# Pinning every instruction of a planned recurrence to the order in which its planner emitted it

## The chip, the cores and the metric

The kernel runs on one core of one Trainium2 chip. The metric is the device time of the program in microseconds (us), lower is better. One core has TensorE (PE, matmuls; PEld are its weight loads), VectorE (DVE), ScalarE (ACT), GpSimd (POOL) and SyncE (SP), which here issues the DMAs. Each engine takes its instructions from one queue of its own, one after the other; an instruction that needs something from another engine waits on a semaphore at the head of its queue.

## The reference

A two-layer backbone over 512 latent tokens with 256 context tokens ahead of them, model width 1024. Layer 0 mixes with mLSTM and gated linear attention, layer 1 with a bidirectional RWKV-7, and each layer ends in a gated convolutional FFN. The part of the kernel that the change touches is the RWKV-7 mixing:

```python
def rwkv_project(h, shifted, mu, w_rkv, ...):
    xx = shifted - h
    xr, xw, xk, xv, xa, xg = (h + xx * mu[i] for i in range(6))
    r = xr @ w_rkv[0];  k = xk @ w_rkv[1];  v = xv @ w_rkv[2]
    ...
def step(S, inp):                       # one token of one head, 64x64 state
    rt, wt, kt, vt, kkt, at = inp
    sa = einsum("bhvk,bhk->bhv", S, -kkt)
    S = S * wt[:, :, None, :] + sa[..., None] * (kkt * at)[:, :, None, :] + vt[..., None] * kt[:, :, None, :]
    return S, einsum("bhvk,bhk->bhv", S, rt)
```

16 heads of 64 channels, 768 tokens, once forward and once backward; the latent scan starts from the state that the context left.

## The kernel before, in words

Up to line 1309 `rwkv_mixer` projects v, the low-rank terms and r on TensorE, in three products of split operands each (`dense`: weight high half by token high half, high by low, low by high). From line 1314 on `self.nc` is a `Meter`, and all that follows to line 1427 is emitted through it. This stretch is called the recurrence here.

Its work is cut into threads, each a Python generator:

- `kp0` to `kp7` (line 1273, called K0 to K7 below) are the eight output blocks of the k projection. They begin with eight rounds in which DVE makes `vt`, ACT casts it to `vh` and DVE subtracts for `vl` (the token halves; line 1275), then `unit` loads a block's weights (`wraw`, a DMA), ACT casts them to `whi` and DVE (even blocks) or POOL (odd ones) subtracts for `wlo` (lines 1277 and 1280, one block ahead). The products are `pk`; ACT copies them to `pv`, and a DMA stores them to `dk`.
- `shared p` (line 1438) prepares pair p of heads: it loads `k`, `v`, `r` and makes `kk`, `a`, `P0`, `P1` and the bonus `bv`; its products are `pn`, `pa`, `pkb`, `pbo`.
- A unit u is one pair in one direction (16 units, u = 2p and 2p + 1). `prep` (line 1571; `pw`, then `ps`) makes the decays and the chunk products `T1`, part of which goes through DRAM (`dx`). `leaf` (line 1712) loads it back and inverts 16x16 triangles by 30 short DVE instructions in a row, stores the result (`dqi`) and loads it as `q0t`. `feed` (line 1660, `ps`) and `values` (line 1685, `pvt`) prepare operands.
- `trans` (line 1744, three per unit) are dense products on `q0t` and `T1`: `pmg`, `pmy`, `pmt`, with ACT and DVE copies between.
- `rec` (line 1821) is the serial chain: 11 steps, each two `cst` products, then one `SU` on ACT and one on DVE, which the next step needs; then 16 `yps` products.
- `close` finishes a pair. `wo` (line 1395) starts the output projection for the first six pairs, block m = 0 to 7, and `fill` (`mod_fill`) makes eight blocks of the modulation vectors; both are there to be put between the rest. Their products are `wo` and `mfill`.

`flow` (line 214) decides in which order the threads emit: it keeps a time for each thread, takes the earliest, lets it emit to its next `yield`, and the `Meter` reckons from its own table of costs (line 180), its record of which buffers are written and read, and the time at which each engine is free, when that piece ends. PSUM banks are handed out the same way. So the order of emission is a list schedule by the `Meter`'s costs.

That order is not yet the order of the queues. The kernel is built in a tile framework whose scheduler goes over all instructions of the program, in order of emission as priority, with a cost model of its own: where it reckons that the next instruction of an engine isn't ready, it issues a later one that is. It may also move an instruction of the recurrence ahead of earlier parts of the program. Instructions are recorded at one line, 210, since all pass through `MeterEngine.call`; the tile names tell them apart.

Of the kernel before, what the change touches and what calls it, by code (L numbers as in the profile page):

```python
# [102 lines left out]
class Meter:  # L103
# [2 lines left out]

    SEM = 0.1

    def __init__(self, nc):
        self.nc, self.eng, self.mode = nc, {}, None  # L110
        self.free = dict(tensor=0.0, vector=0.0, scalar=0.0, gpsimd=0.0, sync=0.0)
        self.wr, self.rd = {}, {}
        self.avail = dict(L=[0.0] * 2, C=[0.0] * 2, R=[0.0] * 4)
        self.begin()
# [4 lines left out]
    def __getattr__(self, name):  # L119
        if name in self.free:  # L120
            return self.eng.setdefault(name, MeterEngine(self, name))
        return getattr(self.nc, name)
# [77 lines left out]
class MeterEngine:  # L200
# [3 lines left out]
    def __getattr__(self, op):  # L204
        f = getattr(getattr(self.meter.nc, self.name), op)

        def call(*a, **k):
            aps = [x for x in list(a) + list(k.values()) if isinstance(x, bass.AP)]
            self.meter.record(self.name, op, aps[0], aps[1:])
            return f(*a, **k)  # L210
        return call


# [57 lines left out]
class Net:  # L271
# [954 lines left out]
    def rwkv_mixer(self, hf, xd, norms=None, post=lambda *a: None):  # L1226
        nc, I = self.nc, self.I
# [83 lines left out]
        small = (uw, ua, ug, blk, half)  # L1311
        st = [dict(dirs=[{}, {}], ys=[None]) for _ in range(NC)]
        zh, zl, y = [None] * NC, [None] * NC, []
        meter = self.nc = Meter(nc)
        zero = self.sl("zero", 780)
        nc.gpsimd.memset(zero, 0.0)

# [755 lines left out]
```

## Time and profile before

| | |
|---|---|
| median of 3 runs | 2827.05 us (2825.29 to 2833.61) |
| the profiled execution | 2823.43 us, span 2821.7 us |
| mean granted TensorE clock | 0.937 |
| busy share of the span | PE 90%, DVE 57%, ACT 37%, POOL 39% |
| recurrence, first to last instruction of PE | about 1462 to 2357 us of the span |

"Busy" is the union of an engine's instructions. A view by windows gives the busy time of each engine in a stretch, the granted clock (1.00 is full) and the number of instructions. In a timeline a row has start, duration, engine, line, operation, tiles, shapes, and in brackets how long the engine had been idle and what it had waited for. The view of waits lists who waited for whom, with total, times and longest.

### The profile page before, as it was taken

What the parts mean: (1) busy time and instruction counts of PE and PEld (TensorE: products, weight loads), DVE (VectorE), ACT (ScalarE), POOL (GpSimd) and SP (SyncE); (2) the same over time, 40 slices, a digit from 0 to 9 for tenths busy, and PEclk for the clock granted to TensorE, in tenths of its full rate; (3) what the DMA queues carried; (4) which work ended last, traced back from release to release, by engine and by line L of the source; (5) the groups of instructions that cost most, each with busy time, mean ns of one, the idle gap of its engine ahead of it and who ended that gap; (6) DMA issues with size and microseconds to landing.
All of it is one profiled execution on the core that took longest, in us unless ns stands there. A gap on an engine that the chain in (4) does not pass through costs nothing.

```text
span 2821.7 us, 47085 instructions
## 1 busy us (share of the span) xinstructions
PE 2543.4 (90%) x19012; PEld 2064.8 (73%) x19012; DVE 1599.1 (57%) x2855; ACT 1056.2 (37%) x2205; POOL 1089.5 (39%) x1115
## 2 busy tenths in 40 slices
PE   5889999888899999986998969989998898989997
PEld 2677777778788888886766756767776677877777
DVE  4567756635535364457464265765666635555655
ACT  4543433445333232233442223434433334343332
POOL 2443445445333333435212133333323214464544
PEclk8999999989999999997999989999998998999999
DMA  6222233342121212221342222223122123232222
GB/s 225 67 83 74 64 131 120 111 142 83 49 63 55 63 56 68 75 98 59 113 134 73 88 63 55 75 61 76 47 57 47 33 73 120 71 95 81 90 77 97
DMA packets 186194, 233.59 MB, mean 83 GB/s; under 512 B 110840, under 2 KB 126584, under 8 KB 185976
## 3 DMA queue, kind: packets, MB, share of 16 engines
q1 hardware_dynamic: 185976, 230.58, 27.1%
q8 instruction: 149, 2.44, 0.4%
q14 instruction: 69, 0.57, 0.1%
HBM read 201.03 MB, written 29.51 MB: 82 GB/s over the span
## 4 chain that ended last, share of the span: by engine, by line
PE 27%; DVE 12%; DMA 4%; issue 3%; ACT 3%; POOL 2%; SPq 0%; POOLq 0%; DVEq 0%; ACTq 0%
DVE fa L1085 6%; PE pmg L210 4%; PE pmy L210 2%; PE ps L210 2%; PE pmt L210 2%; DVE leaf L210 2%; PE pk L210 2%; PE mfill L210 2%; PE cst L210 2%; PE wo L210 1%; PE pdL L373 1%; PE pdL L377 1%; PE pdL L374 1%; DMA wraw<-in_down 1%; POOL wlo L362 1%
## 5 line engine op out<-in xcount | busy, mean ns | idle before, releaser
L362 POOL TENSOR_TENSOR wlo<-wraw,whi 128x512 fp32r<-128x512 f32 (+1 forms) x469 | 643.3, 1388 | 836.7 <-ACT whi L361 667.8
L1085 DVE SCALAR_TENSOR_TENSOR fa<-pl,vec,fa 128x512 f32<-128x512 f32 x352 | 352.0, 1013 | 287.2 <-ACT fa L1083 276.4
L361 ACT CAST whi<-wraw 128x512 fp32r<-128x512 f32 (+1 forms) x529 | 296.9, 599 | 426.8 <-DMA wraw<-in_up 189.7
L210 POOL TENSOR_SCALAR_AFFINE_SELECT T<-T 64x256 f32<-64x256 f32 x192 | 100.7, 528 | 119.3 <-ACT T L210 72.1
L373 PE MATMUL pdL<-gh,whi 128*128 128x512 f32 x288 | 116.0, 403 | 16.4 <-DVE y L1142 11.6
L373 PE MATMUL pjL<-zh,whi 128*128 128x512 f32 x304 | 120.5, 396 | 4.6 <-DVE fa L1088 4.6
L373 PE MATMUL pjL<-mh,whi 128*128 128x512 f32 x304 | 120.6, 397 | 1.5 <-DVE fa L1088 1.5
L374 PE MATMUL pjL<-ml,whi 128*128 128x512 f32 x304 | 120.9, 398 | 0.0
L374 PE MATMUL pdL<-gl,whi 128*128 128x512 f32 x288 | 115.4, 401 | 5.9 <-POOL gl L1103 3.1
L374 PE MATMUL pjL<-zl,whi 128*128 128x512 f32 x304 | 120.6, 397 | 0.0
L377 PE MATMUL pjL<-mh,wlo 128*128 128x512 f32 x304 | 120.4, 396 | 0.0
L377 PE MATMUL pjL<-zh,wlo 128*128 128x512 f32 x304 | 119.8, 395 | 0.0
L1086 ACT ACTIVATE fa<-fa 128x256 f32<-128x256 f32 (+1 forms) x66 | 36.9, 560 | 213.6 <-DVE fa L1085 213.5
L377 PE MATMUL pdL<-gh,wlo 128*128 128x512 f32 x288 | 115.2, 400 | 0.0
L210 PE MATMUL pmy<-T,q0t 64*64 64x192 f32 x768 | 101.7, 360 | 1.2 <-DVE kk L210 0.8
L210 POOL TENSOR_TENSOR rn<-rn,powc 128x12 f32<-128x12 f32 (+1 forms) x16 | 31.3, 1959 | 180.5 <-DVE rn L210 169.8
L1142 DVE TENSOR_TENSOR y<-y,pdL 128x512 f32<-128x512 f32 x48 | 32.8, 686 | 111.9 <-PE pdL L377 111.9
L210 DVE TENSOR_SCALAR SU<-cst,el 64x64 f32<-64x64 f32 x176 | 51.1, 291 | 78.4 <-PE cst L210 73.3
L373 PE MATMUL pjC<-mh,whi 128*128 128x256 f32 x304 | 86.0, 283 | 9.5 <-DVE fa L1088 9.5
L210 ACT ACTIVATE SU<-cst,el 64x64 f32<-64x64 f32 x176 | 54.2, 308 | 106.2 <-PE cst L210 104.4
L210 ACT COPY T<-pmy 128x384 f32<-128x384 f32 x96 | 44.7, 477 | 115.2 <-PE pmy L210 106.0
L374 PE MATMUL pjC<-ml,whi 128*128 128x256 f32 x304 | 85.5, 281 | 0.0
(501 smaller groups left out, 7458.5 us busy)
## 6 DMA issues: line engine op xcount, KB each, us to landing
wraw<-in_up SPq DMA_DIRECT2D x88, 512.0 KB, 3.6
wraw<-in_wmod SPq DMA_DIRECT2D x64, 512.0 KB, 4.2
wfill<-in_wmod SPq DMA_DIRECT2D x32, 512.0 KB, 4.5
wraw<-in_rkv SPq DMA_DIRECT2D x24, 512.0 KB, 4.0
wraw<-in_win_fm SPq DMA_DIRECT2D x21, 512.0 KB, 3.9
wraw<-in_down SPq DMA_DIRECT2D x32, 320.0 KB, 2.9
xd<-y SPq DMA_DIRECT2D x64, 128.0 KB, 1.8
wraw<-in_down SPq DMA_DIRECT2D x32, 256.0 KB, 2.6
```

The source lines that it names most:

```text
L210: return f(*a, **k)
L361: nc.scalar.copy(hi[:, c], raw[:, c])
L362: (nc.gpsimd if lo == "pool" else nc.vector).tensor_tensor(w[:, c], raw[:, c], hi[:, c].bitcast(F32), op=ALU.subtract)
L373: nc.tensor.matmul(pst[tag][:m, :w], w1, xh[kc][:, o:o + w], start=st, stop=False)
L374: nc.tensor.matmul(pst[tag][:m, :w], w1, xl[kc][:, o:o + w], start=False, stop=False)
L377: nc.tensor.matmul(pst[tag][:m, :w], w0, xh[kc][:, o:o + w], start=False, stop=sp)
L1085: nc.vector.scalar_tensor_tensor(b, src, fw(f, i), b, op0=ALU.mult, op1=ALU.add)
L1086: nc.scalar.activation(a, a, AF.Gelu_apprx_tanh)
L1142: nc.vector.tensor_tensor(yj, yj, pst[tag][:, :w], op=ALU.add)
```

## The change

`MeterEngine.call` passes every instruction to the framework's `keep_in_program_order`, and the `Meter` gets the framework's context for that.

```diff
-    def __init__(self, nc):
-        self.nc, self.eng, self.mode = nc, {}, None
+    def __init__(self, nc, tc):
+        self.nc, self.tc, self.eng, self.mode = nc, tc, {}, None
...
             self.meter.record(self.name, op, aps[0], aps[1:])
-            return f(*a, **k)
+            return self.meter.tc.keep_in_program_order(f(*a, **k))
...
-        meter = self.nc = Meter(nc)
+        meter = self.nc = Meter(nc, self.tc)
```

That function adds a dependency without a semaphore from the instruction to the one that was emitted last before it on the same engine:

```python
    prev = next((i for i in reversed(cur.bb.instructions)
                 if i is not ins.ins and i.engine == engine), None)
    if prev is not None:
        self.add_manual_dep(ins.ins, prev.name, DependencyInfo(NoSync, DATA), reason="keep_in_program_order")
    return ins
```

So within the recurrence each of the five queues, SP's DMAs among them, stands in the order of `flow`, and its first instruction on each engine stands behind all that was emitted last before it there. No instruction is added or taken away, and the emission order is the same. What is emitted ahead of line 1314 or behind line 1427 isn't pinned.

## Prediction

> **What bounds the kernel now.** I read the page's first rows, then the recurrence by windows, one for each stage of it, then the timelines of PE, DVE, ACT and POOL at its two ends, then the waits. The columns behind the stretch are its length, then busy time of PE, PEld, DVE, ACT and POOL with counts, the granted clock, the DMA share and GB/s.
>
> ```profile
> span 2821.7 us, 47085 instructions
> ...
> 1461.00:1490.00 29.00, 27.81 (x125) 16.85 (x124) 17.62 (x21) 10.80 (x17) 5.40 (x4) 1.00 0.37 120
> 1490.00:1553.00 63.00, 52.52 (x306) 38.01 (x304) 27.83 (x57) 16.13 (x32) 18.99 (x24) 0.92 0.30 85
> 1553.00:1611.00 58.00, 57.29 (x569) 45.64 (x570) 9.95 (x25) 14.26 (x36) 3.48 (x6) 0.94 0.22 76
> 1611.00:1636.00 25.00, 19.40 (x150) 12.40 (x148) 11.37 (x26) 9.34 (x18) 14.11 (x25) 1.00 0.54 149
> 1636.00:1650.00 14.00, 3.78 (x4) 1.17 (x4) 13.39 (x30) 0.83 (x2) 5.69 (x6) 0.51 0.00 1
> 1650.00:1664.00 14.00, 7.70 (x66) 6.74 (x67) 7.22 (x13) 2.80 (x6) 1.18 (x1) 0.63 0.22 36
> 1664.00:2258.00 594.00, 542.55 (x7184) 415.80 (x7180) 384.41 (x983) 232.77 (x551) 195.77 (x328) 0.94 0.24 57
> 2258.00:2357.00 99.00, 97.59 (x1005) 73.90 (x1006) 32.30 (x67) 39.12 (x91) 21.66 (x20) 0.97 0.28 82
> 1461.00:2357.00 896.00, 808.64 (x9400) 610.51 (x9399) 504.10 (x1219) 326.05 (x749) 266.28 (x414) 0.93 0.26 66
> ```
>
> PE is busy in 808.6 of the recurrence's 896 us. Its idle time, 87.4 us, is all that another order could win there, and it lies unevenly: 1.2 us in the first 29, where the k projection starts, 10.5 in the next stage, 0.7 up to 1611, 22.1 around unit 1 (1611 to 1664), 51.5 in the 594 us of the middle, 1.4 at the end. What PE waits for, when it waits, is in the view of waits:
>
> ```profile
> PE pmg L210 <- DMA q0t<-dqi: 23.4, 5, 7.7
> PE pbo L210 <- DVE bv L210: 14.3, 2, 12.0
> ```
>
> The columns are the total in us, the count and the longest. Three of the five waits of the first row, at the first products of units 0, 1 and 15:
>
> ```profile
> 1553.30 0.29 PE L210 MATMUL pmg<-q0t,T 64*64 64x64 f32 x2 [2.05 <-DMA q0t<-dqi]
> 1656.30 0.44 PE L210 MATMUL pmg<-q0t,T 64*64 64x64 f32 x2 [7.17 <-DMA q0t<-dqi]
> 2258.49 0.44 PE L210 MATMUL pmg<-q0t,T 64*64 64x64 f32 x2 [7.67 <-DMA q0t<-dqi]
> ```
>
> So the two ends run almost without a gap now, and what the scheduler did there by leaving the planner's order can only be lost; in the middle there is something to win.
>
> **The start: the k projection behind its own operands.** The queue of ACT, from the last low-rank instruction on, before:
>
> ```order
> L1292 ACTIVATE ug<-prL 128x512
> L210 CAST vh<-vt 128x768
> L210 CAST whi<-wraw 128x512 x2
> L210 CAST vh<-vt 128x768 x2
> L210 CAST whi<-wraw 128x512 x2
> L210 CAST vh<-vt 128x768 x4
> ```
>
> and now:
>
> ```order
> L1292 ACTIVATE ug<-prL 128x512
> L210 CAST vh<-vt 128x768 x8
> L210 CAST whi<-wraw 128x512 x4
> L210 COPY pv<-pk 128x512
> L210 COPY pv<-pk 128x256
> ```
>
> All eight token casts now stand ahead of the first weight cast, and on DVE likewise all eight `vt` and `vl` stand ahead of the first `wlo`. In before the first weights had been split long ahead, among the r projection. On PE nothing is left to pass the time, before:
>
> ```order
> L377 MATMUL prL<-rh,wlo 128x512
> L210 MATMUL mfill<-wfill,cth 2x512 x3
> L210 MATMUL pk<-vh,whi 128x512
> L210 MATMUL pk<-vh,whi 128x256
> L210 MATMUL pk<-vl,whi 128x512
> ```
>
> and now:
>
> ```order
> L377 MATMUL prL<-rh,wlo 128x512
> L210 MATMUL pk<-vh,whi 128x512
> L210 MATMUL pk<-vl,whi 128x512
> L210 MATMUL pk<-vh,whi 128x256
> L210 MATMUL pk<-vl,whi 128x256
> L210 MATMUL pk<-vh,wlo 128x512
> L210 MATMUL pk<-vh,wlo 128x256
> L210 MATMUL mfill<-wfill,cth 2x512
> ```
>
> The fills, and the block K1 that ran beside K0, stand behind K0's products. The durations of this stretch:
>
> ```profile
> 1461.81 0.40 PE L377 MATMUL prL<-rh,wlo 128*128 128x512 f32 x1
> 1462.14 2.31 PE L210 MATMUL mfill<-wfill,cth 128*2 128x512 f32 x5
> 1462.87 0.43 DVE L1293 TENSOR_SCALAR ug<-ug 128x512 f32<-128x512 f32 x1 [0.51 <-ACT ug L1292]
> 1473.77 1.28 DVE L210 TENSOR_TENSOR wlo<-wraw,whi 128x512 fp32r<-128x512 f32 x2
> 1478.62 1.01 DVE L210 SCALAR_TENSOR_TENSOR vt<-xx,vec,y 128x768 f32<-128x768 f32 x1
> 1480.54 0.96 DVE L210 TENSOR_TENSOR vl<-vt,vh 128x768 fp32r<-128x768 f32 x1 [0.91 <-ACT vh L210]
> 1481.42 1.01 DVE L210 SCALAR_TENSOR_TENSOR vt<-xx,vec,y 128x768 f32<-128x768 f32 x1
> 1466.89 1.14 ACT L210 CAST whi<-wraw 128x512 fp32r<-128x512 f32 x2 [3.33 <-DMA wraw<-in_rkv]
> 1489.73 0.86 ACT L210 COPY pv<-pk 128x512 f32<-128x512 f32 x2 [3.44 <-PE pk L210]
> 1594.78 5.45 PE pk L210 x30
> 1549.62 3.54 DMA q0t<-dqi
> ```
>
> A round `vt`, `vh`, `vl` takes 1481.42 - 1478.62 = 2.80 us, since DVE waits for ACT in it. The first round starts behind `ug`, at 1463.3; eight end at 1485.7, `vh` of the last about 1.0 earlier. The first half of `whi` is there at 1485.3, and of `wlo` at 1486.3. PE, done at 1462.2, has its first product at 1485.3: 23 us with nothing, where before it was busy. K0 is then 48 products at 5.45 / 30 = 0.18 us, 8.7, and two fills between them, each two passes of 2.31 / 5, 1.8. With 0.4 of waiting for `wlo` that makes 1496.2. To it comes the clock: after PE's idle stretch around unit 1 the granted clock stayed low, 0.63 on the mean of 1650 to 1664, so (1 - 0.63) x 14 / 0.5 = 10.4 us at half rate; 6.3 of them PE was idle, in 4.1 it worked at half, which costs 2. K0 ends at 1498.2 instead of 1489.7, 8.5 us late. (The Trainium skill, "TensorE: Matmul & The Clock Gate", section "What's actually happening", says that the array falls to half rate after an idle window of about 3.4 us and comes back after as long a busy one; by that alone the clock would cost 1.7 us, and the sum be 0.3 lower.)
>
> What hides a loss of PE time, other work, isn't there: pair 0's chain hangs on K0 and ran from 1489.7 to 1553.2, where `q0t` of unit 0 lands. Two things lengthen it. The weights of block 2 are now loaded behind the store of K0, and their split stands on DVE ahead of `kk`: 0 to 2 us, I take 0.5. The split of block 4 and `feed`'s and `values`' copies stand ahead of unit 0's leaf: 0 to 4, I take 2. So unit 0's products start 11 us late.
>
> From there to the end of K7 PE was busy in 57.3 of 58 us. It now has more to do there, a quarter of K4 (12 products, 2.2) and five fills (4.6), put off from before; of these 6.8 I let 4 count, as the products also wait for copies in gaps too short to show as idle. That is 15 at K7, and unit 1 starts behind it in the old order as in the new.
>
> **Unit 1.** Its leaf ran broken up by `bv` of the pair, with PE held at `pbo`:
>
> ```profile
> 1643.63 0.73 DVE L210 SCALAR_TENSOR_TENSOR bv<-r,vec,P 64x512 f32<-64x512 f32 x1
> 1644.54 0.75 DVE L210 SCALAR_TENSOR_TENSOR bv<-r,vec,P 64x512 f32<-64x512 f32 x1
> 1648.22 0.68 DVE L210 TENSOR_TENSOR bv<-pbo,v 128x512 f32<-128x512 f32 x1
> ```
>
> All three now stand behind the leaf, which ends 0.73 + 0.75 + 0.68 = 2.2 us sooner. I take 2 back: 13 at the first products of unit 1. Between 7 and 18 are possible, by the ends above and the short gaps.
>
> **The middle.** Here the two orders differ only around the odd units' chain and the even units' first products. The difference on PE where unit 1's chain meets unit 2 (`T_13583` and `T_13584` are two groups of it):
>
> ```order
>  L210 MATMUL mfill<-wfill,cth 2x512
> -L210 MATMUL cst<-SU,mgl 64x64
> +L210 MATMUL cst<-SU,mgl 64x64 x8
> +L210 MATMUL pmg<-q0t,T_13583 64x64 x8
> +L210 MATMUL pmy<-T_13583,q0t 64x192 x8
>  L210 MATMUL mfill<-wfill,cth 2x512
> +L210 MATMUL pmg<-q0t,T_13584 64x64 x8
> +L210 MATMUL pmy<-T_13584,q0t 64x192 x8
>  L210 MATMUL cst<-SU,mgl 64x64 x2
> -L210 MATMUL pmg<-q0t,T_13583 64x64
> -L210 MATMUL pmy<-T_13583,q0t 64x192
> ```
>
> The scheduler had put single products on `q0t` into the chain, where they could hold PE, and fills between its steps; now four steps stand in a row. Both have a price in before:
>
> ```profile
> 2240.61 0.33 PE L210 MATMUL cst<-SU,gm 128*64 128x64 f32 x2 [0.39 <-ACT SU L210]
> 2241.34 0.33 PE L210 MATMUL cst<-SU,mgl 128*64 128x64 f32 x2 [0.40 <-ACT SU L210]
> ```
>
> A step in a row leaves PE idle for 0.4 us. I count some 20 such steps that had other work between them and now have none: 8 us. Against that stand the waits for `q0t`. Units 1's and 15's, 7.2 and 7.7 us, came where nothing else was left, and stay, and 2.1 is unit 0's; the other 6.5 may go, and with them the 2.3 that `pbo` cost elsewhere (14.3 - 12.0): I take 9. Net 1 back. The ends are 12 worse (all steps, and leaves that wait for a chain step placed ahead of them on DVE) and 15 better (half of the 30 us that are idle without a wait that stays).
>
> **The end.** `wo`'s weights had been split ahead; now, on ACT, each block's cast stands behind the copy of the block before, and POOL's or DVE's half behind that:
>
> ```profile
> 2353.01 0.59 ACT L210 COPY y<-wo 128x512 f32<-128x512 f32 x1 [0.18 <-PE wo L210]
> 2337.73 0.92 ACT L210 CAST whi<-wraw 128x384 fp32r<-128x384 f32 x2
> 2338.37 1.97 POOL L210 TENSOR_TENSOR wlo<-wraw,whi 128x384 fp32r<-128x384 f32 x2 [10.17 <-ACT whi L210]
> ```
>
> From a block's last product to the next one's third, which needs `wlo`: 0.59 + 0.46 + 0.98 = 2.0 us. Six borders make 12; the first three lie beside chain steps that hide about all but 0.5, the last three beside nothing but `close`. I take 5 (2 to 9).
>
> The sum: 2823.4 of the profiled execution + 13 - 1 + 5 = 2840.4. The median lies 3.6 above that execution, which gives 2844.
>
> **The rivals.** *Paid back*: the pinned order removes PE's blocked products in full, 23.4 + 14.3, and hides the fills it saved up in the chain. With 18 of the 38 us back in place of 1, it comes to 2827, between 2822 and 2832. For it: the middle's 51.5 idle us; against: most of that is a leaf arriving late, which no order of PE changes. *Faster*: the same with 30 us back: 2815; from 26.5 us on it passes the bound below. Against it stands that 14.9 of `q0t`'s waits have nothing to put in their place. *Much slower*: the chain's DVE steps now stand between blocks of six leaf instructions (up to 2 us each), and PE stands in order behind the chain. At 4 us for each of eight pairs this adds 32: 2876. *The change does nothing* is ruled out by the order above.
>
> **How the numbers follow.** 0.3% of 2827, 8.5 us, is what a measurement of this kernel can tell from no change. Forecast 0.62, own range 2834 to 2860; paid back 0.20; faster 0.12; much slower 0.06. The range from 2822 to 2862 leaves out the last two. Slower by more than 8.5 takes the forecast and the last rival, 0.68; same 0.20.
>
> **What would show it.** After: PE idle for about 23 us from 1462 on, with a low clock behind it; K0's `pv` near 1498, unit 0's first `pmg` near 1564, K7's last product near 1625; the middle as long as before; gaps of 1 to 2 us between blocks of `wo`. I am wrong if that gap is under 10 us, if unit 1's first `pmg` comes within 5 us of 1656, or if the middle shrinks or grows by over 15.

## The result, and the profile after

The changed kernel takes 2858.78 us (median of 4 runs, 2858.47 to 2866.58), the kernel before 2826.77 us (median of 4, 2825.29 to 2833.61). The ratio is 1.0115, 95% interval 1.0091 to 1.0139: slower by 32.0 us. The forecast was 2844, slower by 17, with a range of 2834 to 2860: the direction came as forecast, the size nearly twice, just inside the range. The profiled execution is one of 2858.47 us, with a span of 2856.7 us.

To compare the traces I cut them at the same instructions of PE: the last `prL` of the r projection, the last `pk` of K0, the first `pmg` of unit 0, the last `pk` of K7, the first `pmg` of units 1 and 15, the last `yps` of unit 15, the last `wo`, and the end of the span. The lengths between them in us, each from one profiled execution (all runs of the sections below are in it; "all" is the sum of the second to eighth column, the recurrence):

```
                r end  K0   unit 0  K7   unit 1  unit 15  rec15  wo   rest   all
before         1462.2 27.6   63.5  57.6   45.4    618.8   64.4  17.7  464.6  894.9
changed        1459.3 36.3   68.4  64.1   48.9    622.9   62.9  24.0  469.8  927.6
start_free     1470.2 28.0   64.0  57.6   51.8    621.8   63.1  24.0  469.8  910.2
wo_free        1453.6 36.6   70.2  64.0   52.0    622.3   58.1  17.6  466.9  920.9
middle_only    1462.6 28.3   63.4  57.6   52.1    622.3   58.2  17.7  464.4  899.6
weights_first  1454.7 32.6   69.9  62.1   50.7    629.0   58.9  24.6  470.5  927.9
pe_only        1463.4 25.8   65.3  61.9   49.5    611.9   62.6  17.6  466.3  894.6
pe_free        1454.4 36.2   67.3  56.3   45.1    619.0   63.9  25.8  466.8  913.6
dve_act        1460.0 36.4   67.2  57.2   42.7    609.4   63.8  24.4  469.9  901.1
fill_free      1450.0 36.6   72.4  62.3   46.9    614.0   63.0  25.5  467.8  920.7
late_only      1461.3 27.7   63.8  57.6   45.1    623.4   58.2  17.6  466.4  893.5
pe_late        1462.5 27.4   64.1  57.6   46.8    624.7   58.2  17.6  464.7  896.5
pe_late_nofill 1464.6 27.7   63.9  57.6   45.5    611.7   58.2  17.7  466.8  882.4
late_nofill    1462.9 27.6   64.1  57.7   44.9    617.1   58.1  17.7  466.1  887.2
```

The changed recurrence is 32.7 us longer: 20.1 up to K7 (8.7, 4.9 and 6.5), 3.5 around unit 1, 4.1 in the middle (unit 1's to unit 15's first product), -1.5 in the last pair, 6.3 in `wo`'s tail (each rounded). Behind it come another 5.2. The first column, ahead of the recurrence, differs between executions for no reason that the change gives (last section), so stages are compared by length.

The start, on PE, with the wait in brackets as before:

```profile
1458.92 0.39 PE L377 MATMUL prL<-rh,wlo 128*128 128x512 f32 x1
1482.31 0.80 PE L210 MATMUL pk<-vh,whi 128*128 128x512 f32 x1 [23.01 <-ACT whi L210]
...
1486.33 0.80 PE L210 MATMUL pk<-vh,whi 128*128 128x512 f32 x1
1486.92 0.63 PE L210 MATMUL pk<-vl,whi 128*128 128x512 f32 x1
...
1488.02 0.40 PE L210 MATMUL pk<-vh,whi 128*128 128x512 f32 x1
```

and on ACT, where the last of eight token casts stands ahead of the weights' casts:

```profile
1480.91 0.83 ACT L210 CAST vh<-vt 128x768 fp32r<-128x768 f32 x1 [1.95 <-DVE vt L210]
1481.65 2.18 ACT L210 CAST whi<-wraw 128x512 fp32r<-128x512 f32 x4
1495.53 0.86 ACT L210 COPY pv<-pk 128x512 f32<-128x512 f32 x2 [11.71 <-PE pk L210]
```

PE stands still for 23.0 us where it worked before. Its first products then take 0.80 us instead of 0.40, until 1487: half rate for about 4.9 us (granted clock 0.50 from 1482.3 to 1487.2). K0's copy follows at 1495.5, 36.6 behind the last `prL`'s start. The start, the stretch around unit 1, the middle and the tail by windows (columns as before: length, busy PE, PEld, DVE, ACT, POOL, clock, DMA share, GB/s):

```profile
1459.00:1496.00 37.00, 13.99 (x56) 8.69 (x54) 16.73 (x19) 10.14 (x16) 3.44 (x5) 0.68 0.24 85
...
1628.00:1677.00 49.00, 26.00 (x156) 14.28 (x154) 25.32 (x53) 10.87 (x20) 14.73 (x22) 0.76 0.32 79
1677.00:2300.00 623.00, 552.53 (x7487) 425.20 (x7489) 408.89 (x1005) 244.84 (x571) 196.80 (x335) 0.92 0.26 60
...
2363.00:2387.00 24.00, 18.55 (x81) 13.19 (x82) 4.48 (x8) 7.11 (x15) 9.34 (x8) 1.00 0.52 175
```

Against the 1.2 us of before, PE is now idle for 23.0 in the first row; in the row of unit 1 it is idle for 23.0, about as before; in `wo`'s tail for 5.5, where it had hardly a gap.

What PE waits for in the whole recurrence now:

```profile
PE cst L210 <- DVE SU L210: 30.6, 19, 3.8
PE pk L210 <- ACT whi L210: 23.0, 1, 23.0
PE pbo L210 <- DVE bv L210: 17.1, 2, 14.4
PE cst L210 <- ACT SU L210: 14.0, 25, 2.3
PE wo L210 <- ACT whi L210: 5.7, 5, 2.1
PE pmg L210 <- DMA q0t<-dqi: 3.9, 2, 3.0
PE ps L210 <- DVE mgl L210: 1.8, 2, 1.1
```

The same rows of the kernel before:

```profile
PE ps L210 <- DVE mgl L210: 9.5, 9, 3.2
PE cst L210 <- DVE SU L210: 9.3, 10, 2.5
PE cst L210 <- ACT SU L210: 2.9, 8, 0.4
```

The wait for `q0t`, 23.4 in before, has shrunk to 3.9, all of it unit 0's; units 1 and 14 wait for it no longer. In exchange the wait of the chain's `cst` for its own state has grown from 12.2 to 44.6 us.

Around unit 1 on PE, first two rows of the kernel before, then the changed one:

```profile
1613.29 4.45 PE L210 MATMUL mfill<-wfill,cth 128*2 128x512 f32 x10
1620.30 4.12 PE L210 MATMUL ps<-bk,av 64*64 64x192 f32 x48 [0.59 <-DVE bk L210]
```

```profile
1637.38 5.94 PE L210 MATMUL ps<-bk,av 64*64 64x192 f32 x48 [5.86 <-DVE bk L210]
1670.16 2.04 PE L210 MATMUL pbo<-bv,blk 128*128 128x512 f32 x2 [14.39 <-DVE bv L210]
1672.13 1.87 PE L210 MATMUL mfill<-wfill,cth 128*2 128x512 f32 x2
1673.93 2.19 PE L210 MATMUL pw<-uw,wsm 128*128 128x512 f32 x4
1676.06 1.05 PE L210 MATMUL mfill<-sel,frow 2*128 2x2 f32 x8
1677.04 0.68 PE L210 MATMUL pmg<-q0t,T 64*64 64x64 f32 x16
```

and SP, whose two loads of `q0t` took 3.6 us each to land:

```profile
1671.34 1.29 SPq L210 DMA_DIRECT2D q0t<-dqi  x2
```

`q0t` is there at about 1671.99 + 3.6 = 1675.6 (the second load is issued some 0.65 behind the first, half of the row's 1.29), but PE, held at `pbo` until `bv` behind the leaf, then has a fill, `pw` and a row of fills ahead of unit 1's first product, most of it at half rate: 1677.0.

### The profile page after: what moved, and what is told of

Same layout as the page of the kernel before. It is cut to its first block, busy times and chain, and to the rows that moved or that the text cites. A ratio compares the mean times of both kernels' runs of the same rounds, so it can differ in the third digit from the quotient of the medians.

```text
span 2856.7 us, 47134 instructions
## 1 busy us (share of the span) xinstructions
PE 2528.4 (89%) x19012; PEld 2048.2 (72%) x19012; DVE 1608.1 (56%) x2855; ACT 1059.0 (37%) x2205; POOL 1081.2 (38%) x1115
## 4 chain that ended last, share of the span: by engine, by line
PE 29%; DVE 14%; ACT 3%; issue 2%; POOL 2%; DMA 1%; POOLq 0%; SPq 0%; ACTq 0%; DVEq 0%
DVE fa L1085 6%; PE pmg L210 4%; PE ps L210 3%; DVE leaf L210 3%; PE pmt L210 3%; PE mfill L210 2%; PE pk L210 2%; PE pmy L210 2%; PE cst L210 1%; PE wo L210 1%; PE pdL L373 1%; PE pdL L374 1%; PE pdL L377 1%; DVE SU L210 1%; PE pw L210 1%
## 5 line engine op out<-in xcount | busy, mean ns | idle before, releaser
L377 PE MATMUL pjC<-mh,wlo 128*128 128x256 f32 x304 | 85.1, 280 | 0.0
L210 DVE TENSOR_TENSOR leaf<-leaf 96x169 f32<-96x169 f32 (+14 forms) x240 | 78.2, 326 | 7.3
```

What stands on the lines that cost most here:

```text
L210: return self.meter.tc.keep_in_program_order(f(*a, **k))
L377: nc.tensor.matmul(pst[tag][:m, :w], w0, xh[kc][:, o:o + w], start=False, stop=sp)
```

## The experiments

All but one (`weights_first`) keep the planner's emission and change only which instructions are pinned. `flow` notes the thread that emits and those that are done, and `call` asks a condition:

```diff
+        meter.cur, meter.done = name, done
         x = next(g, None)
...
-            return self.meter.tc.keep_in_program_order(f(*a, **k))
+            i = f(*a, **k)
+            return self.meter.tc.keep_in_program_order(i) if COND else i
```

An instruction that is pinned behind one that isn't still stands behind it. Each run was timed against the kernel before on its own chip; the ratio is to that.

### The places: start, tail, middle

`start_free`:

```diff
+ COND: "kp7" in self.meter.done
```

> Nothing is pinned until the last block K7 of the k projection has been emitted; from there on every instruction is pinned as in the changed kernel. My theory (the loss is a sum of separate places, and the start's 17.2 us at K7, 20.1 counted from the end of the r projection, is carried to the end in full): PE without a gap over 2 us at the start, K7 done near 1611, unit 1's first product near 1660, and about 2858.8 - 20 = 2839 us. Rival (the pairs of units have a pace of their own, set by the pinned middle, and the start's lateness would have been absorbed): 2852 to 2859.

Measured: 1.0058 (1.0040 to 1.0075), median 2847.0. Up to K7 the stages are those of before, 149.6 in place of 168.8; the recurrence is 910.2, shorter by 17.4. Of the 19.2 us that are gone at K7 all but 1.8 are gone at the end, and the rival with a pace of its own falls. (The forecast of 2839 was 8 too low; 3.6 of that is the chip, on which the kernel before took 2830.3.) The stretch around unit 1 grew to 51.8, though, and the rest stayed: the start is not all.

`wo_free`:

```diff
+ COND: self.meter.cur != "wo"
```

> Everything is pinned but the thread of wo (its loads, splits, products and copies). My theory: the gaps between wo's blocks go (6.3 us of the changed kernel), and with ACT and POOL free earlier the up projection's splits start inside the recurrence again, which wins part of the 5 us lost behind it: 2848 to 2853 us, the start as in the changed kernel. Rival (PE at the tail is held by the last units' chain and by close, so that wo's splits are hidden anyway): 2857 to 2860.

Measured: 1.0054 (1.0033 to 1.0074), median 2845.8. The tail is back at 17.6, the last pair is 4.8 shorter (58.1), the rest 2.9 shorter: 9.6 by the trace, with unit 1's stretch 3.1 longer and the time below my 2848 to 2853. The ratio says 17 (1.0115 - 1.0054 of 2827), and both ratios have some 6 us of uncertainty, so the two agree within it; I go by the trace. The rival of hidden splits falls. The rows of the changed kernel's tail show the wait:

```profile
2376.12 0.50 PE L210 MATMUL wo<-zh,whi 128*128 128x512 f32 x1 [2.13 <-ACT whi L210]
2381.78 0.50 PE L210 MATMUL wo<-zh,whi 128*128 128x512 f32 x1 [1.09 <-ACT whi L210]
2382.92 0.50 PE L210 MATMUL wo<-zh,wlo 128*128 128x512 f32 x1 [0.41 <-POOL wlo L210]
```

and ACT between them, a block's `whi` behind the copy of the block before, and the next stage's splits (line 361) only behind that:

```profile
2380.73 0.58 ACT L210 COPY y<-wo 128x512 f32<-128x512 f32 x1 [4.25 <-PE wo L210]
2381.21 0.93 ACT L210 CAST whi<-wraw 128x384 fp32r<-128x384 f32 x2
2382.03 1.14 ACT L361 CAST whi<-wraw 128x512 fp32r<-128x512 f32 x2
```

`middle_only`:

```diff
+ COND: "kp7" in self.meter.done and self.meter.cur != "wo"
```

> Pinned only from the end of the k projection on, and without the wo thread: the pinned middle alone. My theory (a sum of places): 2827 + 3.5 between K7 and unit 1 + 4 in the middle, 2832 to 2837 us, with the waits for the chain's state at about 45 us in the middle as in the changed kernel (13 in the kernel before). Rival (the pinned middle is a gain that the start hid): under 2824. Second rival (pinned chain steps cost most of the 32 us): 2845 or more.

Measured: 0.9999 (0.9982 to 1.0016). The two places together hold the whole loss that can be measured. By the trace the pinned remainder costs 4.7: 6.7 around unit 1 and 3.5 in the middle, 6.2 back in the last pair. The waits of `cst` are 44.4 us there, as forecast, and the time is that of before all the same, 2 to 7 us below my 2832 to 2837: the second rival falls.

### What the start is made of

`weights_first` (all pinned):

```diff
-            kh, kl = pairs(2, 0)
             lo = lambda p: "pool" if p % 2 else "dve"
             us = [self.unit(I["rkv"][1, 0], lo(0))]
+            kh, kl = pairs(2, 0)
```

> All is pinned, but the first weight block of the k projection is loaded and split ahead of the eight token splits instead of behind them. My theory: PE's first product comes near 1463 + 4 in place of 1482, K0 then goes at the pace of the token splits, 2.8 us each, and ends near 1488 in place of 1495.6; some 7 of the start's loss goes: about 2852 us. Rival (with a product only every few hundred ns the clock stays low for longer, and K0 and K1 run at half rate for longer): K7 not earlier by more than 3, 2856 to 2860.

Measured: 1.0094 (1.0067 to 1.0122), median 2856.3. PE's first product comes 9.1 us behind the r projection in place of 23.0, since `whi` now waits 4.7 us for its load, and `wlo` and the first token round come behind it; K0 goes at the pace of the token splits, and its end comes only 3.7 earlier, K7's 4.2. The recurrence is as long as before this edit, 927.9. It isn't a clean test of the rest: the edit moves the planner's emission, and the order of PE's products in the middle is another one than the changed kernel's. Rows of PE:

```profile
1463.73 0.80 PE L210 MATMUL pk<-vh,whi 128*128 128x512 f32 x1 [9.07 <-ACT vh L210]
1472.09 0.50 PE L210 MATMUL pk<-vh,whi 128*128 128x512 f32 x1 [0.63 <-ACT vh L210]
1480.50 0.79 PE L210 MATMUL pk<-vh,whi 128*128 128x512 f32 x1 [0.70 <-ACT vh L210]
```

The 0.80, 0.50 and 0.79 show the clock going up and down in K0; its mean from the r projection's end to K0's end is 0.74. My step held as a mechanism; the gain of 7 was too large, and by K7 the rival's 3 is nearer than my 7.

`pe_only`, `pe_free` and `dve_act`:

```diff
+ pe_only   COND: self.name == "tensor"
+ pe_free   COND: self.name != "tensor"
+ dve_act   COND: self.name in ("vector", "scalar")
```

> Only TensorE's instructions are pinned; DVE, ACT, POOL and SP are the scheduler's again. My theory (the start's loss needs both: the weights split behind all token splits on ACT and DVE, and PE with nothing but K0 ahead): the 23 us of waiting shrink to a pace of 2.8 us a token split, K0 ends 28 us after the r projection (36.3 in the changed kernel, 27.6 before), K7 some 160 us after it (168.8, 148.7), no gaps in wo's tail: 1.004 to 1.007 of the kernel before, about 2842 us. Rival (the loss is PE's order as such, its products stand in a row behind the chain): 1.010 or more. Second rival (the loss is the order on the other engines): under 1.002.

> All engines are pinned but TensorE. My theory: since ACT and DVE stand in the changed kernel's order, PE has nothing to do at the start whatever its own order, so its 23 us of waiting for the first weights stay, and wo's late splits too: 1.008 to 1.011 of the kernel before, about 2853 us. Rival (PE's order makes the loss): 1.004 or less.

> Only DVE's and ACT's instructions are pinned. My theory (the start's loss is that the weights' splits stand behind all token splits on these two engines, the tail's that each whi cast stands behind the copy of the block before): 30 to 37 us from the end of the r projection to K0's end as with all pinned (27.6 before, 36.3 changed), wo's last stretch 24 to 26 us (17.7 before), 1.004 to 1.008 of the kernel before. Rival (SP's loads or POOL's halves standing in line make it): K0's end within 29 us, 1.002 or less.

Measured: `pe_only` 0.9997 (0.9982 to 1.0012), `pe_free` 1.0047 (1.0028 to 1.0066), `dve_act` 1.0015 (0.9999 to 1.0032), all together 1.0115. With PE alone pinned, K0 runs at the pace of the splits and ends 25.8 us behind the r projection, 1.8 sooner than before, because K1's products no longer share PE with it:

```profile
1464.76 0.50 PE L210 MATMUL pk<-vh,whi 128*128 128x512 f32 x1 [1.41 <-ACT vh L210]
1469.60 0.50 PE L210 MATMUL pk<-vh,whi 128*128 128x512 f32 x1 [1.82 <-ACT vh L210]
1472.53 0.79 PE L210 MATMUL pk<-vh,whi 128*128 128x512 f32 x1 [0.72 <-ACT vh L210]
```

K7 comes 4.3 late (153.0), unit 1's stretch is 4.1 longer, and the middle, 611.9, gives 6.9 back. My forecast for this run, 1.004 to 1.007, was wrong: the middle's gain was not in it. The time is the second rival's, under 1.002. With PE free and the rest pinned the 23 us of waiting stay, K0 at 36.2, as I expected, but PE catches up 9 of the start's 20 by K7 (159.8) and all around unit 1 (45.1); the ratio, 1.0047, lies between the two forecasts and nearer to the rival's. `dve_act` shows that ACT and DVE alone make the start's wait (36.4) and the tail's (24.4), as forecast; its time, though, is the rival's, because its stretch around unit 1 (42.7) and its middle (609.4) are together 12 shorter than before. So neither queue order is the whole loss: PE's alone costs nothing that can be measured, and that of all the others 1.0047 of the 1.0115. I read it so: the other engines' order makes the lateness, and PE's fixed order keeps it from being filled.

### What the middle is made of

`fill_free` and `late_only`:

```diff
+ fill_free   COND: self.meter.cur != "fill"
+ late_only   COND: "leaf1" in self.meter.done and self.meter.cur != "wo"
```

> Everything is pinned but the fill thread (products of a weight row that wait for nothing but their load). My theory: the fills go into the gaps of the chain and of unit 1's leaf as in the kernel before, but the waits themselves stay, the start's too, and fills only moved: PE idle in the recurrence a few us less than 136, time 1.009 to 1.011 of the kernel before. Rival (the fills kept PE and its clock busy through the start's and unit 1's stalls, and their being pinned is most of the loss): K0's products at full rate from the first, 1.006 or less.

> Pinned only from the end of unit 1's leaf on, without the wo thread: the k projection, pair 0, unit 1's preparation and the tail's weights are the scheduler's. My theory: the stretch from K7 to unit 1's first product, 45.4 us before and 52.1 when pinned from K7 on, returns to 45 to 46; the middle stays 3.5 longer, the last pair 6 shorter; the recurrence 891 to 896 us (894.9 before), the time 0.997 to 1.001 of the kernel before. Rival (the stretch is longer because of pair 1's order, which is still pinned): the recurrence at 899 or more, 1.000 to 1.003.

Measured: `fill_free` 1.0070 (1.0049 to 1.0090), below my 1.009. K0 is as late as ever (36.6): the fills did not go into the start's wait, so the rival's reason falls too. They won 8.9 in the middle, 2.0 around unit 1, 1.8 up to K7, and lost 4.0 ahead of unit 0. `late_only` 0.9996 (0.9978 to 1.0014): the stretch around unit 1 is 45.1 again, as I said, the middle 623.4, the recurrence 893.5. Pinning from that point on costs nothing and wins nothing.

`pe_late`, `pe_late_nofill` and `late_nofill`:

```diff
+ pe_late         COND: self.name == "tensor" and "leaf1" in self.meter.done and self.meter.cur != "wo"
+ pe_late_nofill  COND: the same, with self.meter.cur not in ("wo", "fill")
+ late_nofill     COND: "leaf1" in self.meter.done and self.meter.cur not in ("wo", "fill")
```

> Only TensorE pinned, from the end of unit 1's leaf on, without the wo thread. My theory (PE's order alone wins 7 us between unit 1's and unit 15's first products, 611.9 with PE alone pinned against 618.8, and cost 4 to 9 at the start and unit 1, where the scheduler's order is now kept): the recurrence 886 to 889 us (894.9 before), 0.996 to 0.998 of the kernel before. Rival (that gain was only a late start caught up in pairs that have a pace of their own): the recurrence 893 to 897, 0.999 to 1.001.

> As the run before, with the fills left to the scheduler too. My theory (fills in the chain's gaps and the chain's steps in a row each win some 7 to 9 us in the middle, and only partly the same ones): the middle 606 to 612 us, the recurrence 882 to 889, 0.994 to 0.998 of the kernel before. Rival (the gains are one and the same): equal to the run before within 2 us of the recurrence.

> All engines pinned from the end of unit 1's leaf on, without the wo thread and without the fills. My theory (the free fills won 8.9 us of the middle with all the rest pinned, 614.0 against 622.9): the middle 613 to 616 us in place of 623.4, the recurrence 884 to 888, 0.995 to 0.998 of the kernel before. Rival (that gain came from the lateness of unit 1 being caught up): the middle 620 or more, the recurrence 891 or more.

Measured: `pe_late` 0.9983 (0.9965 to 1.0000): its middle is 624.7, not 612. My theory that PE's order alone wins 7 us there falls: in their middles the two kernels have the same order on PE but for 6 of some 7,480 products, and need 611.9 and 624.7. The recurrence, 896.5, is the rival's (a late start caught up); what exactly `pe_only` won stays open. `pe_late_nofill` 0.9936 (0.9912 to 0.9961), median 2813.2: faster than both kernels, with a middle of 611.7 and a recurrence of 882.4. `late_nofill` 0.9949 (0.9929 to 0.9969), with a middle of 617.1, a little longer than my 613 to 616, and a recurrence of 887.2. In both pairs the only difference is whether the fills are pinned, and it is worth 13.0 and 6.3 us of the middle. The waits of PE in the middle, first `pe_late`, then `pe_late_nofill`:

```profile
PE cst L211 <- DVE SU L211: 20.0, 28, 3.9
PE pmg L211 <- DMA q0t<-dqi: 11.2, 6, 5.7
PE cst L211 <- ACT SU L211: 9.4, 21, 1.3
```

```profile
PE cst L211 <- DVE SU L211: 15.1, 20, 2.0
PE pmg L211 <- DMA q0t<-dqi: 14.9, 7, 6.5
PE cst L211 <- ACT SU L211: 4.1, 9, 0.7
```

The middle holds 40 of the 64 fills in both. Freed, more of them lie between the chain's steps: of their 80 passes 38 stand directly between two `cst` in place of 10. The chain's waits fall from 29.4 to 19.2 us, those for `q0t` rise by 3.7; PE is idle for 8.1 us less in all, and busy for 4.9 less.

## Why the prediction was right in direction and half in size

By terms, forecast and measured: 15 and 20.1 us up to K7; -2 and 3.5 around unit 1; -1 and 2.6 in the middle with the last pair; 5 and 6.3 in the tail; nothing and 5.2 behind the recurrence. The stretch ahead took 2.9 less in this execution. So the kind of each place was foreseen but for unit 1 and the stretch behind, and nearly every size was too small.

**The start: right to K0, too small behind it.** The wait of 23 us was forecast and is 23.0, from the row of the token rounds. K0's end was put 8.5 late and is 8.7 late, counted from the r projection's end. The clock had been taken at 10.4 us of half rate, 4.1 of them in work; the work at half rate lasted about 4.9. (The Trainium skill, "TensorE: Matmul & The Clock Gate", section "What's actually happening", puts the return of the full rate after about 3.4 us of work and says that the point varies; what the trace shows is longer than its figure and than the sum's term, and costs 2.4 us in place of 1.7 or 2.) Behind K0 the sum counted 2.5 more to unit 0 and 4 to K7; the trace has 4.9 and 6.5. Ahead of unit 0's leaf DVE does stand at the copies of `feed` and `values` that were named:

```profile
1548.98 0.29 DVE L210 COPY SU<-pvt 64x128 f32<-64x128 f32 x1 [0.33 <-ACT SU L210]
```

The leaf follows at 1549.2, 2.3 us behind the landing of its data, close to the 2 that I took for it. What was too low is the 0.5 for the way there: the data land 51.3 us behind K0 in place of 47.4. The last `bk` is already 2.5 late by then; which place in a queue costs that wasn't followed. The leaf then takes 8.2 us in place of 9.8 and ends 4.6 late. Up to K7 the put-off work is there: 156 products of the k projection in place of 144, and five fills more. PE is busy for 4.7 us more, close to the 4 that I let count; what the sum lacked is 1.9 us of waits, for `q0t` and in the chain. That unit 0's first product came at 1564.0, the very time forecast, is chance: this execution reached the recurrence 2.9 us sooner. `start_free` confirms the size of the whole: it wins 17.4 us.

**Unit 1: the sign was wrong.** The step read "all three now stand behind the leaf, which ends 2.2 us sooner. I take 2 back". From its first instruction to its last the leaf is indeed shorter, 16.1 before (1633.9 to 1650.0) and 13.3 now (1655.3 to 1668.6). But it starts 27.2 behind K7 in place of 23.0. Its data have landed by 1650.1, no later behind K7 than before; on DVE, though, a `kk` that waits for `pkb` now stands ahead of it:

```profile
1653.55 1.02 DVE L210 TENSOR_TENSOR kk<-kk,pkb 128x512 f32<-128x512 f32 x2 [1.22 <-PE pkb L210]
```

On PE `pkb` comes 24.2 behind K7 in place of 20.4. Ahead of it the kernel before had spent the wait for `bk` on five fills; now, behind one fill, PE stands idle for 5.9 us and then takes 5.94 in place of 4.12 for the 48 products of `ps`, at a granted clock of 0.69 in place of 1.00. And the work that I let go behind the leaf, `bv` and with it `pbo`, came back on PE: `pbo`, a fill, `pw` and the row of fills stand ahead of unit 1's first product, which comes 8.4 behind the leaf's end in place of 6.3, and no longer waits for `q0t`. So -2 became 4.2 - 2.8 + 2.1 = 3.5. These causes are read from the rows; none was tested by itself. In every kernel whose PE is pinned here with the fills, the stretch is 48.9 to 52.1, with the fills free 46.9, and with PE free or pinned only later 42.7 to 46.8: the stretch is long only where PE's order is fixed; that of the other engines alone doesn't make it so.

**The middle: two errors that cancelled, nearly.** I took 8 worse for chain steps in a row and 9 better for waits that go: net 1 back; measured 2.6 worse with the last pair, 4.1 without. More steps than the 20 forecast came to wait: the waits of `cst` on `SU` went from 18 to 44. Their price was further off: 0.4 us was that of one row at the end, the mean of the 44 is 44.6 / 44 = 1.0, and 32 us of waits came in place of 8. Between the first products of units 1 and 15, the stretch of the table, the chain's waits grew by 31.1. Against them the waits for `q0t` (unit 14's too, which I held for certain) fell by 14.2 and those of `ps` for `mgl` by 7.7; other waits grew by 9 in all. So PE is idle for 18.3 us more, 70.5 in place of 52.2. That this costs only 4.1 comes from a term that the sum didn't have: for the same products PE is busy 14.1 us less, 552.5 (in the table by windows above) in place of 566.6:

```profile
1656.30:2275.10 618.80, 566.62 (x7484) 436.97 (x7486) 391.05 (x999) 239.60 (x566) 198.22 (x330) 0.93 0.25 59
```

The group whose busy time shrank most is one of those that the scheduler had strewn singly into the chain, the `pmy` products on `q0t`. A view by groups has the count, the busy time of the group in us, the mean in ns, and the idle time before it; before, then changed:

```profile
L210 PE MATMUL pmy<-T,q0t 64*64 64x192 f32 x672 | 88.8, 360 | 0.8 <-DVE kk L210 0.8
L210 PE MATMUL pmy<-T,q0t 64*64 64x192 f32 x672 | 65.1, 333 | 3.1 <-DVE J L210 2.9
```

That their place in the order is why they took longer was not tested by itself.

(The prediction calls the wait at 2258.49 unit 15's; it is the first product of unit 14. No term hangs on the name.)

**The tail: right in kind, a little low, and not the end of it.** 5 was forecast, with 2 to 9; it is 6.3, with gaps of 1.1 and 2.1 us in the rows above. (The prices that the prediction gives for the six borders, three at 0.5 and three at 2.0, add up to 7.5; why it took 5 it doesn't say.) What the sum lacked is the stretch behind the recurrence, 5.2 longer. There the next stage's weight splits (lines 361 and 362), which the scheduler had put into the recurrence's end from 2344.6 on, start behind `wo`'s. On ACT before:

```profile
2344.55 1.66 ACT L361 CAST whi<-wraw 128x512 fp32r<-128x512 f32 x3
```

`wo_free` brings 2.9 of it back and `middle_only` all. Eight of these casts start on ACT ahead of `wo`'s last product in the kernel before, and two in the changed one. The kernels with two, those with ACT pinned to the end, `wo` included, range from +2.2 to +5.9 here; those with eight from -0.2 to +2.3. That these splits are the cause is read from this, and not tested by itself.

**The rivals.** "Paid back" and "faster" hung on the middle's blocked products; they are blocked no more, and the chain took the time. "Much slower" had the right waits, the chain's, and they grew by 32 us; that its own 32, eight pairs at 4 us, is the same figure is chance, and it left out that nearly as much would go elsewhere.

## What to carry to other kernels

A planner's emission order is a plan for the engines together. In this kernel the scheduler behind it repaired what the plan had wrong where the plan begins and ends most of all, where it could reach into the neighbouring stages for work. Before pinning an order, look at its first and last microseconds on each engine, and leave free whatever waits for nothing (here the fills): pinned, it can't fill the gap that opens somewhere else than planned. Where a pinned serial step is priced, use at least the mean wait of that step over the stage, not the shortest row: before it was 12.2 / 18 = 0.7 us here against the 0.4 that I took, and even that would have been too low.

## What the runs showed of the hardware

The stretch ahead of the recurrence has the same order of products on PE in all fourteen kernels, and took between 1450.0 and 1470.2 us in their profiled executions; the kernel before alone ranged from 2812.7 to 2840.2 us over these sessions. So a difference of 5 us between two kernels can't be read from single times. I read it from the lengths of stages, which repeat better: from K0's end to K7's they took 121.0 to 121.8 us in all seven kernels with that part left to the scheduler.

Two of the leaf's short instructions, 96x1 and 96x4, took 1.75 and 1.65 us where POOL worked beside them. On DVE, first the 96x1 alone in the kernel before, then the two in the changed one:

```profile
1633.91 0.15 DVE L210 TENSOR_TENSOR leaf<-leaf 96x1 f32<-96x1 f32 x1 [2.52 <-DMA leaf<-dx]
1655.32 1.75 DVE L210 TENSOR_TENSOR leaf<-leaf 96x1 f32<-96x1 f32 x1
1657.29 1.65 DVE L210 TENSOR_TENSOR leaf<-leaf 96x4 f32<-96x4 f32 x1
```

and on POOL:

```profile
1655.07 3.86 POOL L210 TENSOR_TENSOR P<-kk,a 64x768 f32<-64x768 f32 x2
```

They end within 0.02 us of the two `P`, at 1657.07 and 1658.94. The kernel before has the same further on in the leaf, where a leaf instruction took 1.65 and one on `a` 2.09 us in place of 0.92, so little of the difference can come from it.
